# First MLP matrix as a Strassen product of seven blocks, its squares sent through DRAM to the second matrix

## The chip, the cores and the metric

One core of a Trainium2 chip runs one program that holds the whole block of the network. The metric is the time of one execution in microseconds, the median of several. The engines have the names of the profile: PE (TensorE, matmuls), DVE (VectorE), ACT (ScalarE), POOL (GpSimd) and SP (SyncE, which issues the DMAs here).

## What is computed

A diffusion block over 1,024 tokens of width 1,024: a mixer (attention beside a state-space layer), its out-projection added to x, and then the part that is changed, a modulated norm and an MLP of width 4,096 with squared ReLU. From the reference:

```python
def sq_relu_mlp(h, w1, b1, w2, b2):
    return jnp.square(jax.nn.relu(h @ w1 + b1)) @ w2 + b2
...
        x = x + g1_l * mix_l
        h2_l = modulate(rms_norm(x, norm2_g[l]), sh2_l, sc2_l)
        x = x + g2_l * sq_relu_mlp(h2_l, w_mlp1[l], b_mlp1[l], w_mlp2[l], b_mlp2[l])
```

All inputs are float32: `w_mlp1` is 1024x4096, `w_mlp2` 4096x1024. The modulation vectors come from `silu(c) @ w_mod`, of which `g2`, the gate of the MLP, is the last.

## The kernel before

**Precision.** Each float32 matrix product is made of three matmuls of a rounded type: an operand is split into a rounded part H (an ACT copy into the type fp32r) and the rest L (raw minus H, on POOL or DVE), and the products H·H, H·L and L·H are summed in one PSUM bank (`mm3`, L139–145). `wload` (L119) brings a 128x1024 block of weights into one of three raw buffers `wr`, and `wtile` (L124–137) splits it into `wH` and `wL`, four buffers each; with `scale_row` DVE first multiplies the raw block by the gate (L134). There are six PSUM banks for products (`mmc`) and two for transposes (`trc`).

**Out-projection and norm.** The loop at L1550–1579 makes x += merged @ w_out for eight token tiles, in two halves n of 512 columns. In its second half, behind the first three token tiles, stand four calls of `mod2` (L1246–1265); eight of the ten calls for one vector stream a 512 KB block of `w_mod` each, multiplied by a per-partition column on DVE (L1253, L1255) into the accumulator `m2a`; the last two add the bias and sum over partitions. `norm2(f)` (L1528) normalises tokens 512f to 512f+511 and `mod_h2` (L1539–1547) transposes them, eight groups of four 128x128 blocks, applies scale and shift, and splits into `h2H`, `h2L`.

**MLP.** Row block ft is 128 of the 4,096 hidden units. `mlp1_half(ft, w, f)` makes hidden units of ft for one half f of the tokens: 24 matmuls of 128x512 (eight contraction blocks, three terms), ReLU and square on ACT, the square again on DVE for the low part (L1607), its split on POOL (L1608). The squares stay in SBUF. `mlp1_first` runs row blocks 0 to 3 on the first half of the tokens while the second half is transposed. `mlp2(b)` multiplies the squares of two row blocks by the rows of w2, in sixteen PSUM groups of six matmuls, and DVE adds each group to x (L1645). After `mlp1_first`, `mlp1(b)` and `mlp2(b-1)` alternate. Each matrix has 1,536 matmuls of 128x512.

**Order.** The code is written in program order; the tool that builds the program puts instructions on each engine in an order of its own from the dependences and the buffers, and each engine runs its list in order. All DMAs, loads and stores, are issued by SP, in one list. A pool's tile waits for the last reader of the buffer it takes over.

Of the kernel before, what the change touches and what calls it, by code (L numbers as in the profile page):

```python
# [48 lines left out]
def block_kernel(ctx, tc, io, out, dbg=None):  # L49
# [1455 lines left out]
    x2p = ctx.enter_context(pool("x2p", reuse_waits="tile"))  # L1505
    x2 = [x2p.tile([128, 1024], F32, name=f"x2{t}") for t in range(8)]
    gb2 = x2p.tile([128, 1024], F32, name="gb2")
    LD.dma_start(gb2, bcast_rows(io["b_mlp2"], 1024))
    h2H, h2L = {}, {}

    def h2_tiles(p, f):
        for k in range(8):
            h2H[k, f] = p.tile([128, 512], F32R, name=f"h2H{k}{f}")
            h2L[k, f] = p.tile([128, 512], F32R, name=f"h2L{k}{f}")

    h2_tiles(ctx.enter_context(pool("h2a", reuse_waits="tile")), 0)
    n2 = ctx.enter_context(pool("n2", reuse_waits="tile"))
# [21 lines left out]
    def mod_h2(f, ks):  # L1539
        for k in ks:  # L1540
            p = trc()
            for i in range(4):
                T.transpose(p[:, i * 128:(i + 1) * 128], xs[4 * f + i][:, k * 128:(k + 1) * 128], ident)
            S.activation(h2H[k, f], p, AF.Identity, bias=sh2[:, k:k + 1], scale=sc2[:, k:k + 1])
            hf = n2.tile([128, 512], F32, name="hf", tag="hf", bufs=2)
            V.tensor_scalar(hf, p, sc2[:, k:k + 1], sh2[:, k:k + 1], op0=OP.mult, op1=OP.add)
            (V if k % 2 else G).tensor_tensor(h2L[k, f], hf, h2H[k, f], op=OP.subtract)

    m2_todo = list(range(20, 40))
# [60 lines left out]
    def mlp1(b):  # L1610
        for ft in (2 * b, 2 * b + 1):
            w = mlp1_tile(ft)
            for f in range(2):
                mlp1_half(ft, w, f)

    def mlp1_first():

        w = {}
        for ft in range(4):
            w[ft] = mlp1_tile(ft)  # L1620
            mlp1_half(ft, w[ft], 0)
            if ft in (1, 2):
                mod_h2(1, range(4 * ft - 4, 4 * ft))
            if ft < 3:
                for _ in range(2):
                    mod2(m2_todo.pop(0), m2a, m2r, trc)
        LD.dma_start(g2row, bcast_rows(m2_d[3], 1024))
        G.tensor_tensor(gb2, gb2, g2row, op=OP.mult)
        for ft in range(4):
            mlp1_half(ft, w[ft], 1)  # L1630
# [55 lines left out]
```

## Time and profile before

| | us |
|---|---|
| three runs, median (lowest to highest) | 1972.06 (1971.46 to 1973.39) |
| the profiled execution, its own time | 1967.57 |
| its span (first to last instruction) | 1965.6 |
| PE busy in the span | 1879.4 (96%) |
| DVE, POOL, ACT busy | 1262.6 (64%), 937.1 (48%), 641.8 (33%) |
| first MLP1 matmul, counted from the span's start | 1258.78 |
| last addition of MLP2 | 1961.96 |

The rows further below come from the one profiled execution. A busy share says how much of a stretch an engine worked; a timeline row gives start, duration, engine, line, operation, output<-inputs and, in brackets, for how long the engine had been idle before and what released it. PEclk is the granted clock of TensorE as a share of full speed, 2.4 GHz.

### The profile page before, as it was taken

How to read it: one execution, taken by the hardware profiler on the slowest of the kernel's cores; microseconds unless marked ns; L12 is line 12 of the kernel's file. 1: busy time of each engine (PE TensorE's matmuls, PEld its weight loads, DVE VectorE, ACT ScalarE, POOL GpSimd, SP SyncE). 2: the span in 40 equal slices, each digit the busy share in tenths (PEclk: the TensorE clock that was granted, in tenths of full speed). 3: DMA queues.
4: the chain of work that ended last, by engine and by line, in shares of the span. 5: the costliest groups of instructions: out<-in, count | busy, mean ns of one | idle time of the engine just before them, and what ended most of it. 6: DMA issues, size and time to landing. Idle time of an engine off the chain costs nothing.

```text
span 1965.6 us, 23750 instructions
## 1 busy us (share of the span) xinstructions
PE 1879.4 (96%) x8866; PEld 1436.1 (73%) x8866; DVE 1262.6 (64%) x2106; ACT 641.8 (33%) x980; POOL 937.1 (48%) x580
## 2 busy tenths in 40 slices
PE   7879999989899999999989999899999999999999
PEld 4667777778776555555548787778888888888887
DVE  5979999947897787777636455654344444443444
ACT  4552222244314555555551121432222211122220
POOL 2247566623335777777784442453334333334330
PEclk9989999999999999999989999999999999999999
DMA  9321222222222000000007646211111111112102
GB/s 313 80 70 49 74 62 71 75 65 69 79 73 86 17 23 23 22 23 18 23 17 247 213 135 224 65 54 43 57 51 54 43 54 44 43 43 64 44 33 86
DMA packets 144611, 144.00 MB, mean 73 GB/s; under 512 B 25648, under 2 KB 111460, under 8 KB 144496
## 3 DMA queue, kind: packets, MB, share of 16 engines
q1 hardware_dynamic: 144496, 142.48, 23.3%
q8 instruction: 70, 1.15, 0.2%
q14 instruction: 45, 0.37, 0.1%
HBM read 122.87 MB, written 19.45 MB: 72 GB/s over the span
## 4 chain that ended last, share of the span: by engine, by line
PE 66%; DVE 2%; DMA 1%; POOL 1%; issue 1%; ACT 1%; SPq 0%; DVEq 0%; ACTq 0%; POOLq 0%
PE mm L143 14%; PE mm L144 14%; PE mm L145 14%; PE pv L1194 7%; PE sT L1174 4%; PE sT L1177 4%; PE mx L1083 3%; DMA wr<-in_w_mod_dram 1%; PE mm L1560 1%; PE mm L1559 1%; PE mm L1561 1%; PE mx L1088 1%; PE mx L1218 1%; PE mm L210 1%; PE mm L211 1%; PE mm L212 1%
## 5 line engine op out<-in xcount | busy, mean ns | idle before, releaser
L136 POOL TENSOR_TENSOR wL<-wr,wH 128x1024 fp32r<-128x1024 f32 (+1 forms) x120 | 285.3, 2386 | 370.7 <-ACT wH L135 350.3
L135 ACT ACTIVATE wH<-wr 128x1024 fp32r<-128x1024 f32 (+1 forms) x124 | 126.4, 1031 | 597.8 <-PE mm L145 247.1
L1645 DVE TENSOR_TENSOR x<-x,mm 128x512 f32<-128x512 f32 x256 | 173.6, 686 | 166.2 <-PE mm L145 166.2
L1199 POOL TENSOR_TENSOR accP<-accP,P 128x1024 f32<-128x1024 f32 x96 | 240.9, 2509 | 21.0 <-ACT P L1181 15.7
L1085 DVE TENSOR_REDUCE m<-mx 128x1 f32<-128x512 f32 x240 | 154.6, 686 | 76.0 <-PE mx L1083 69.6
L1181 ACT ACTIVATE P<-sT 128x1024 f32<-128x1024 f32 x160 | 163.8, 1027 | 116.2 <-PE sT L1177 110.4
L143 PE MATMUL mm<-h2H,wH 128*128 128x512 f32 x512 | 199.5, 390 | 0.0
L144 PE MATMUL mm<-h2L,wH 128*128 128x512 f32 x512 | 199.4, 389 | 0.0
L145 PE MATMUL mm<-h2H,wL 128*128 128x512 f32 x512 | 199.4, 389 | 0.0
L143 PE MATMUL mm<-wH,sH 128*128 128x512 f32 x512 | 199.2, 389 | 0.0
L144 PE MATMUL mm<-wL,sH 128*128 128x512 f32 x512 | 199.2, 389 | 0.0
L145 PE MATMUL mm<-wH,sL 128*128 128x512 f32 x512 | 199.2, 389 | 0.0
L1608 POOL TENSOR_TENSOR sL<-r,sH 128x512 fp32r<-128x512 f32 x64 | 84.5, 1320 | 165.3 <-DVE r L1607 165.3
L134 DVE TENSOR_TENSOR wr<-wr,g2row 128x1024 f32<-128x1024 f32 x32 | 42.1, 1318 | 171.5 <-DMA wr<-in_w_mlp_dram 171.5
L1194 PE MATMUL pv<-P,Vt 128*64 128x512 f32 x640 | 150.5, 600 | 0.0
L1607 DVE TENSOR_TENSOR r<-r 128x512 f32<-128x512 f32 x64 | 89.1, 1392 | 40.7 <-ACT sH L1606 38.9
L143 PEld LDWEIGHTS mm<-h2H,wH 128*128 128x128 f32 x512 | 96.1, 188 | 20.7 <-issue 0.9
L143 PEld LDWEIGHTS mm<-wH,sH 128*128 128x128 f32 x512 | 96.1, 188 | 19.9
L144 PEld LDWEIGHTS mm<-wL,sH 128*128 128x128 f32 x512 | 96.1, 188 | 19.9
L145 PEld LDWEIGHTS mm<-wH,sL 128*128 128x128 f32 x512 | 96.1, 188 | 19.9
L145 PEld LDWEIGHTS mm<-h2H,wL 128*128 128x128 f32 x512 | 96.1, 188 | 19.8
L144 PEld LDWEIGHTS mm<-h2L,wH 128*128 128x128 f32 x512 | 96.1, 188 | 19.8
(495 smaller groups left out, 4075.2 us busy)
## 6 DMA issues: line engine op xcount, KB each, us to landing
wr<-in_w_mlp_dram SPq DMA_DIRECT2D x64, 512.0 KB
wr<-in_w_in_dram SPq DMA_DIRECT2D x35, 512.0 KB
wr<-in_w_mod_dram SPq DMA_DIRECT2D x32, 512.0 KB
x<-in_x_dram SPq DMA_DIRECT2D x12, 512.0 KB
xt<-in_w_mod_dram SPq DMA_DIRECT2D x24, 256.0 KB
gs_d<-go SPq DMA_DIRECT2D x16, 256.0 KB
q_d<-qo SPq DMA_DIRECT2D x16, 256.0 KB
ql<-q_d SPq DMA_DIRECT2D x16, 256.0 KB
```

Of the source, the lines that this page charges most:

```text
L135: S.activation(H[:, :n], raw[:, :n], AF.Copy)
L136: (low or G).tensor_tensor(L[:, :n], raw[:, :n], H[:, :n], op=OP.subtract)
L143: T.matmul(ps, lH, rH, start=i == 0, stop=False)
L144: T.matmul(ps, lH, rL, start=False, stop=False)
L145: T.matmul(ps, lL, rH, start=False, stop=i == n - 1)
L1085: V.tensor_reduce(m3[:, 4 * j + t, c:c + 1], m, axis=AX.X, op=OP.max)
L1181: S.activation(P, sT, AF.Exp, scale=HD ** -0.5)
L1194: T.matmul(pv[64 * j:64 * j + 64, :], Vt[:, kt, kv * 64:kv * 64 + 64], P[:, j * 512:(j + 1) * 512], start=kt == 0, stop=kt == NK - 1)
L1199: G.tensor_tensor(accP, accP, P, op=OP.add)
L1607: V.tensor_tensor(r, r, r, op=OP.mult)
L1608: G.tensor_tensor(sL[:, o], r, sH[:, o], op=OP.subtract)
L1645: V.tensor_tensor(x2[t][:, o], x2[t][:, o], ps, op=OP.add)
```

## The change

The change replaces the first matrix product by one with seven block products in place of eight. The 1,024 contraction rows are cut in two halves (four blocks of 128 each), and so are tokens (f = 0 and 1) and each pair of row blocks 2p, 2p+1. Of h2 transposed, B11 and B21 are the two contraction halves of the first 512 tokens and B12, B22 those of the second. The kernel makes T1 = B12 − B11, T3 = B22 − B12, T2 = B22 − T1 and T4 = B21 − T2, splits each into H and L, and multiplies each of B11, B21, T2, T1, T3, B22, T4 by a block or a sum of blocks of w1, twelve matmuls each:

- `mod_t(i)` makes B22 and T1 to T4 for contraction block i (i = 0 to 3) in place of `mod_h2(1, ...)`: two transposed groups, then two DVE operations from PSUM, seven on DVE between SBUF tiles, four on POOL and five on ACT. It is called five times, for i = 0 twice.
- `first(p)` makes the products with B11 and B21 of pair p. For p = 0 to 5 they run ahead (NA = 6), between the calls of `mod_t`.
- `mlp1(p)` makes four sums and differences of raw w1 blocks on DVE, splits them, and makes the five other products (60 matmuls; 84 for p ≥ 6, with `first(p)` inside). The four outputs are combined on DVE from PSUM.
- ReLU and square stay on ACT; the squares are stored in DRAM as float32 (`s_d`), read back and split before the second matrix, which now runs after the whole first matrix, in blocks of 1, 3 and then 4 row blocks (`BL`).
- x, stored in DRAM by `norm2` (`x2_d`), is reloaded at the hand-over into tiles that take over the buffers of the first matrix.
- The four `mod2` calls in the out-projection's second half and six behind `mlp1_first` move behind pairs 1 to 5, two each.

```diff
@@ norm2, mod_h2, mod_t
-            dump(f"x2{t}", x2[t])
+            LD.dma_start(x2_d[t], x2[t])
...
+    def mod_t(i):
+        _, b12 = h2_tr(1, i)
+        p, b22 = h2_tr(1, 4 + i)
+        H, L = BO["B22", i]
+        S.activation(H, p, AF.Identity, bias=sh2[:, 4 + i:5 + i], scale=sc2[:, 4 + i:5 + i])
+        G.tensor_tensor(L, b22, H, op=OP.subtract)
+        t1, t2, t3, t4 = (hf_tile() for _ in range(4))
+        (H1, L1), (H2, L2) = BO["B11", i], BO["B21", i]
+        V.tensor_tensor(t1, b12, H1, op=OP.subtract)
+        V.tensor_tensor(t1, t1, L1, op=OP.subtract)
+        G.tensor_tensor(t3, b22, b12, op=OP.subtract)
+        V.tensor_tensor(t2, b22, t1, op=OP.subtract)
+        V.tensor_tensor(t4, H2, t2, op=OP.subtract)
+        V.tensor_tensor(t4, t4, L2, op=OP.add)
+        for nm, t, E in (("T1", t1, G), ("T3", t3, G), ("T2", t2, V), ("T4", t4, V)):
+            H, L = BO[nm, i]
+            S.activation(H, t, AF.Copy)
+            E.tensor_tensor(L, t, H, op=OP.subtract)
...
-            if n == 1 and ts[0] < 3:
-                for _ in range(2):
-                    mod2(m2_todo.pop(0), m2a, m2r, trc)
...
+    def prod(w, h, nm):
+        ps = mmc()
+        wH, wL = w
+        for i in range(4):
+            o = slice(512 * h + 128 * i, 512 * h + 128 * i + 128)
+            bH, bL = BO[nm, i]
+            T.matmul(ps, wH[:, o], bH, start=i == 0, stop=False)
+            T.matmul(ps, wL[:, o], bH, start=False, stop=False)
+            T.matmul(ps, wH[:, o], bL, start=False, stop=i == 3)
+        return ps
...
+    def act_out(r, ft, f):
+        S.activation(r, r, AF.Square)
+        LD.dma_start(s_d[ft][:, f * 512:(f + 1) * 512], r)
+    def c_out(ps, add, ft, f):
+        r = r_tile()
+        V.scalar_tensor_tensor(r, ps, b1(ft), add, op0=OP.add, op1=OP.add)
+        S.activation(r, r, AF.Relu)
+        act_out(r, ft, f)
...
+    def first(p, w):
+        t1s[p] = ml.tile([128, 512], F32, name="t1", tag="t1", bufs=NA)
+        S.activation(t1s[p], prod(w, 0, "B11"), AF.Copy)
+        c_out(prod(w, 1, "B21"), t1s[p], 2 * p, 0)
+    def mlp1(p):
+        r1, r2 = w1_raw(2 * p), w1_raw(2 * p + 1)
...
+        if p >= NA:
+            first(p, wsplit(r1))
+        V.tensor_tensor(cs[:, a], r2[:, a], r2[:, b], op=OP.add)
+        V.tensor_tensor(cs[:, b], cs[:, a], r1[:, a], op=OP.subtract)
+        wc = wsplit(cs)
+        V.tensor_tensor(c4, r1[:, b], cs[:, b], op=OP.subtract)
+        V.tensor_tensor(r2[:, a], r1[:, a], r2[:, a], op=OP.subtract)
+        wr = wsplit(r2)
+        w4 = wsplit(c4, 512)
...
+        V.tensor_tensor(u2, prod(wc, 1, "T2"), t1s.pop(p), op=OP.add)
+        V.tensor_tensor(u4, prod(wc, 0, "T1"), u2, op=OP.add)
+        p7 = prod(wr, 0, "T3")
+        V.tensor_tensor(u3, p7, u2, op=OP.add)
+        c_out(p7, u4, 2 * p + 1, 1)
+        c_out(prod(w4, 0, "B22"), u4, 2 * p, 1)
+        c_out(prod(wr, 1, "T4"), u3, 2 * p + 1, 0)
+    mod_t(0)
+    for p in range(NA):
+        first(p, wsplit(w1_raw(2 * p)))
+        if p in (0, 2, 3):
+            mod_t((0, 0, 1, 2)[p])
+    mod_t(3)
+    m2_todo = list(range(30, 40))
+    for p in range(NP):
+        mlp1(p)
+        if 1 <= p < 6:
+            for _ in range(2):
+                mod2(m2_todo.pop(0), xs4[3], xs4[2], trc)
...
+    pre = [(s_tile(0), w2_tile(0))]
...
+    x2 = [mq.tile([128, 1024], F32, name=f"xr{t}") for t in range(8)]
+    gb2 = mq.tile([128, 1024], F32, name="gb2")
+    for t in range(8):
+        LD.dma_start(x2[t], x2_d[t])
+    LD.dma_start(gb2, bcast_rows(io["b_mlp2"], 1024))
...
+    BL = [[0], [1, 2, 3]] + [list(range(4 * b, 4 * b + 4)) for b in range(1, 8)]
+    for bi, fts in enumerate(BL):
+        tiles = pre if bi == 0 else [mlp2_tiles(ft) for ft in fts]
+        mlp2(fts, tiles, bi == len(BL) - 1)
```

How the lists of the engines move, at three places. First DVE, where the second half of the tokens is built: before, a piece of `mod_h2` between two squares.

```order
L1546 TENSOR_SCALAR hf_10943<-tr_10937,sc2_9068,sh2_9067 128x512
L1607 TENSOR_TENSOR r_10932<-r_10932 128x512
L1546 TENSOR_SCALAR hf_10952<-tr_10946,sc2_9068,sh2_9067 128x512
L1547 TENSOR_TENSOR h2L11_10839<-hf_10952,h2H11_10838 128x512
L1546 TENSOR_SCALAR hf_10961<-tr_10955,sc2_9068,sh2_9067 128x512
L1546 TENSOR_SCALAR hf_10970<-tr_10964,sc2_9068,sh2_9067 128x512
L1547 TENSOR_TENSOR h2L31_10843<-hf_10970,h2H31_10842 128x512
```

In the change, DVE's call for i = 1 (lines of the changed kernel; `hf` are the tiles b12, b22 and t1 to t4, `r` is an output of `c_out`, `wr` a raw block of w1):

```order
L1549 TENSOR_SCALAR hf_11071<-tr_11066,sc2_9068,sh2_9067 128x512
L1579 TENSOR_TENSOR T4L0_10863<-hf_10966,T4H0_10862 128x512
L1570 TENSOR_TENSOR hf_11075<-hf_11064,B11H1_10181 128x512
L1655 SCALAR_TENSOR_TENSOR r_11127<-mm_11114,cols_156,t1_11099 128x512
L1571 TENSOR_TENSOR hf_11075<-hf_11075,B11L1_10182 128x512
L1683 TENSOR_TENSOR wr_11280<-wr_11278,wr_11280 128x512
L1573 TENSOR_TENSOR hf_11076<-hf_11071,hf_11075 128x512
L1574 TENSOR_TENSOR hf_11078<-B21H1_10189,hf_11076 128x512
L1549 TENSOR_SCALAR hf_11137<-tr_11132,sc2_9068,sh2_9067 128x512
L1575 TENSOR_TENSOR hf_11078<-hf_11078,B21L1_10190 128x512
L1579 TENSOR_TENSOR T2L1_10849<-hf_11076,T2H1_10848 128x512
L1549 TENSOR_SCALAR hf_11144<-tr_11139,sc2_9068,sh2_9067 128x512
```

Eight of the twelve operations have both operands in SBUF, where three of seven had. POOL's list beside it, for the same call and up to the first operation of the next:

```order
L1572 TENSOR_TENSOR hf_11077<-hf_11071,hf_11064 128x512
L1567 TENSOR_TENSOR B22L1_10833<-hf_11071,B22H1_10832 128x512
L1579 TENSOR_TENSOR T3L1_10857<-hf_11077,T3H1_10856 128x512
L1579 TENSOR_TENSOR T1L1_10841<-hf_11075,T1H1_10840 128x512
L1663 TENSOR_TENSOR wL_11293<-wr_11280,wH_11292 128x1024
L1663 TENSOR_TENSOR wL_11297<-c4_11283,wH_11296 128x512
L1572 TENSOR_TENSOR hf_11150<-hf_11144,hf_11137 128x512
```

The splits of pair 0's weights (L1663) stand between the calls. Second, DVE in pairs 1 to 5 (`u2`, `u4` and `r` are read from PSUM, `cs`, `c4`, `wr` are sums of raw w1 blocks, L1255 is a modulation product):

```order
L1655 SCALAR_TENSOR_TENSOR r_11453<-mm_11439,cols_156,u4_11410 128x512
L1679 TENSOR_TENSOR cs_11618<-wr_11616 128x512
L1655 SCALAR_TENSOR_TENSOR r_11471<-mm_11458,cols_156,u4_11410 128x512
L1680 TENSOR_TENSOR cs_11618<-cs_11618,wr_11614 128x512
L1683 TENSOR_TENSOR wr_11616<-wr_11614,wr_11616 128x512
L1682 TENSOR_TENSOR c4_11619<-wr_11614,cs_11618 128x512
...
L1255 SCALAR_TENSOR_TENSOR xs3_10201<-wr_11722,sil_157,xs3_10201 128x1024
L1687 TENSOR_TENSOR u2_11522<-mm_11525,t1_11026 128x512
L1255 SCALAR_TENSOR_TENSOR xs3_10201<-wr_11725,sil_157,xs3_10201 128x1024
L1688 TENSOR_TENSOR u4_11524<-mm_11539,u2_11522 128x512
```

The modulation products, which wait for their weights, stand between the additions from PSUM, and the sums of pair 3's weights between the outputs of pair 1. Third, SP at the hand-over. Before, loads of w1 and w2 alternate; now it reads:

```order
L121 DMA wr_13543<-s_d_10873 128x1024
L1648 DMA s_d_10873<-r_13371 128x512
L1648 DMA s_d_10873<-r_13389 128x512
L1648 DMA s_d_10873<-r_13407 128x512
L1726 DMA xr0_13432<-x2_d_10205 128x1024
...
L1726 DMA xr7_13439<-x2_d_10205 128x1024
L1727 DMA gb2_13440<-in_b_mlp2_dram 128x1024
L121 DMA wr_13549<-in_w_mlp2_dram 128x1024
L121 DMA wr_13556<-s_d_10873 128x1024
L121 DMA wr_13562<-in_w_mlp2_dram 128x1024
```

`wr_13543` is square block 2, `wr_13549`, `wr_13556` and `wr_13562` are w2 block 2, square block 3 and w2 block 3; between them stand the last stores of squares and the reload of x.

## Rows read from the trace of the kernel before

**Rows 1.** Page, span and part 1: busy us, share, instructions by engine.

```profile
span 1965.6 us, 23750 instructions
PE 1879.4 (96%) x8866; PEld 1436.1 (73%) x8866; DVE 1262.6 (64%) x2106; ACT 641.8 (33%) x980; POOL 937.1 (48%) x580
```

**Rows 2.** Windows: stretch, us, busy PE PEld DVE ACT POOL, PEclk, DMA share, GB/s.

```profile
1300.00:1964.00 664.00, 661.92 (x2921) 547.94 (x2919) 292.55 (x346) 135.43 (x177) 238.56 (x127) 1.00 0.17 52
1500.00:1900.00 400.00, 400.00 (x1766) 331.31 (x1766) 173.47 (x204) 84.69 (x110) 149.53 (x80) 1.00 0.16 48
1180.00:1190.00 10.00, 10.00 (x46) 8.29 (x45) 3.84 (x6) 0.00 (x0) 0.00 (x0) 1.00 1.02 417
1236.00:1241.00 5.00, 5.00 (x16) 4.10 (x17) 3.22 (x6) 1.45 (x2) 0.00 (x0) 0.50 0.08 23
```

**Rows 3.** Lines by form, 1258 to 1966 us: count, busy us, mean ns, idle before.

```profile
L143 PE MATMUL mm<-h2H,wH 128*128 128x512 f32 x512 | 199.5, 390 | 0.0
...
L1645 DVE TENSOR_TENSOR x<-x,mm 128x512 f32<-128x512 f32 x256 | 173.6, 686 | 166.2 <-PE mm L145 166.2
L136 POOL TENSOR_TENSOR wL<-wr,wH 128x1024 fp32r<-128x1024 f32 x63 | 152.7, 2432 | 187.0 <-ACT wH L135 169.9 <-issue 17.0
...
L135 ACT ACTIVATE wH<-wr 128x1024 fp32r<-128x1024 f32 x61 | 63.2, 1057 | 386.6 <-PE mm L145 247.1 <-PE mm L144 110.1 <-DVE x L1645 19.0
L1604 ACT ACTIVATE r<-mm,cols 128x512 f32<-128x512 f32 x64 | 43.4, 679 | 118.2 <-PE mm L145 118.2
L134 DVE TENSOR_TENSOR wr<-wr,g2row 128x1024 f32<-128x1024 f32 x32 | 42.1, 1318 | 171.5 <-DMA wr<-in_w_mlp_dram 171.5
L1606 ACT ACTIVATE sH<-r 128x512 fp32r<-128x512 f32 x64 | 40.4, 631 | 1.9
```

**Rows 4.** Timeline, start of the MLP: first matmul, second norm, a transposed group.

```profile
1258.78 0.39 PE L143 MATMUL mm<-h2H,wH 128*128 128x512 f32 x1
...
1267.81 2.74 DVE L1536 TENSOR_SCALAR xs<-x,rs 128x1024 f32<-128x1024 f32 x4
...
1272.82 0.60 PE L1543 MATMUL tr<-ident,xs 128*128 128x128 f32 x4
```

**Rows 5.** Timeline, POOL and DVE at 1294 us.

```profile
1294.22 2.39 POOL L1628 TENSOR_TENSOR gb<-gb,g2row 128x1024 f32<-128x1024 f32 x1 [2.99 <-DMA g2row<-m_d]
...
1294.36 2.81 DVE L1607 TENSOR_TENSOR r<-r 128x512 f32<-128x512 f32 x1 [4.49 <-ACT sH L1606]
```

**Rows 6.** One line's operations: ns min/median/max, first and last start.

```profile
L1607 DVE TENSOR_TENSOR r<-r x64: 680/691/2868, 1270.5 to 1920.6; 128x512 f32<-128x512 f32 x64
...
L1547 POOL TENSOR_TENSOR h2L<-hf,h2H x8: 1255/1290/1671, 1241.1 to 1283.6; 128x512 fp32r<-128x512 f32 x8
L1547 DVE TENSOR_TENSOR h2L<-hf,h2H x8: 692/1156/1437, 1241.8 to 1283.9; 128x512 fp32r<-128x512 f32 x8
```

**Rows 7.** Timeline, second half of the out-projection: ACT, DVE, PE at 1228 to 1236.

```profile
1228.51 1.06 ACT L1532 ACTIVATE xs<-x 128x1024 f32<-128x1024 f32 x1 [4.38 <-DVE x L1564]
...
1231.74 1.29 DVE L1255 SCALAR_TENSOR_TENSOR m2a<-wr,sil,m2a 128x1024 f32<-128x1024 f32 x1 [3.26 <-DMA wr<-in_w_mod_dram]
...
1235.92 0.69 PE L1543 MATMUL tr<-ident,xs 128*128 128x128 f32 x2 [5.49 <-DVE xs L1536]
```

**Rows 8.** The chain of waits: a load of w1, start and us.

```profile
1258.26 3.86 DMA wr<-in_w_mlp_dram
```

**Rows 9.** Timeline, SP: the eight loads of x.

```profile
1173.77 5.55 SPq L1525 DMA_DIRECT2D x<-in_x_dram  x8
```

**Rows 10.** Timeline: the last addition.

```profile
1961.96 0.69 DVE L1645 TENSOR_TENSOR x<-x,mm 128x512 f32<-128x512 f32 x1 [0.67 <-PE mm L145]
```

More of the change, by code (lines that the diff above doesn't have):

```diff
@@ L1502, in block_kernel, with b_tiles @@
     man_.__exit__(None, None, None)
[L1505 to L1517, printed above, removed]
+    BO = {}
+    def b_tiles(p, names):
+        for nm in names:
+            for i in range(4):
+                BO[nm, i] = [p.tile([128, 512], F32R, name=f"{nm}{h}{i}") for h in "HL"]
+    h2a_ = pool("h2a", reuse_waits="tile")
+    b_tiles(h2a_.__enter__(), ("B11", "B21"))
+    n2_ = pool("n2", reuse_waits="tile")
+    n2 = n2_.__enter__()
     xs4 = [n2.tile([128, 1024], F32, name=f"xs{i}") for i in range(4)]
@@ L1521, in block_kernel @@
     ts2 = n2.tile([128, 8], F32, name="ts2")
-    m2a = n2.tile([128, 1024], F32, name="m2a")
-    m2r = n2.tile([128, 512], F32, name="m2r")
+    x2_d = dr.tile([8, 128, 1024], F32, name="x2_d")
+    x2p_ = pool("x2p", reuse_waits="tile")
+    x2p = x2p_.__enter__()
+    x2 = [x2p.tile([128, 1024], F32, name=f"x2{t}") for t in range(8)]
     for t in range(8):
@@ L1526, in block_kernel, with hf_tile @@
     xs = {}
+    def hf_tile():
+        return n2.tile([128, 512], F32, name="hf", tag="hf", bufs=6)
     def norm2(f):
@@ L1536, in norm2, with h2_tr, mod_h2 @@
             V.tensor_scalar(xs[t], x2[t], rs2[:, t:t + 1], None, op0=OP.mult)
-            dump(f"x2{t}", x2[t])
-    def mod_h2(f, ks):
-        for k in ks:
[L1541 to L1549, printed above, removed]
+            LD.dma_start(x2_d[t], x2[t])
+    def h2_tr(f, k):
+        p = trc()
+        for i in range(4):
+            T.transpose(p[:, i * 128:(i + 1) * 128], xs[4 * f + i][:, k * 128:(k + 1) * 128], ident)
+        hf = hf_tile()
+        V.tensor_scalar(hf, p, sc2[:, k:k + 1], sh2[:, k:k + 1], op0=OP.mult, op1=OP.add)
+        return p, hf
+    def mod_h2(ks):
+        for k in ks:
+            H, L = BO["B11" if k < 4 else "B21", k % 4]
+            p, hf = h2_tr(0, k)
+            S.activation(H, p, AF.Identity, bias=sh2[:, k:k + 1], scale=sc2[:, k:k + 1])
+            (V if k % 2 else G).tensor_tensor(L, hf, H, op=OP.subtract)
+    def mod_t(i):
[16 more added lines that the diff above has]
+            E.tensor_tensor(L, t, H, op=OP.subtract)
+    m2_todo = list(range(20, 30))
     for n in range(2):
@@ L1610, in mlp1 @@
[L1610 to L1630, printed above, removed]
@@ L1638, in mlp2 @@
+    LD.dma_start(gb2, bcast_rows(io["b_mlp2"], 1024))
+    def mlp2(fts, tiles, last_):
         for t in range(8):
```

98 lines of the change are left out of this document (59 added, 39 removed).

## The prediction

> **What bounds the kernel now.** I first read the page's busy shares: TensorE is busy 96% of the span, no other engine over 64% [rows 1]. An average over stages does not say what the MLP is worth, so next come the windows of its stretch [rows 2]: from 1300 to 1964 us TensorE works 661.9 of 664 us at clock 1.00, VectorE less than half the time, GpSimd a third, DMA a sixth. Both MLP matrices are therefore bound by TensorE, and a matmul fewer saves its whole pitch: 400 us over 1,766 matmuls are **226.5 ns** [rows 2]. The 390 ns of one in the grouped lines [rows 3] is its own length; they overlap, and the pitch counts. The groups [rows 3] give what the side engines pay: VectorE 0.69 us for a 512-wide operation from PSUM, ACT 1.06 and GpSimd 2.43 us for one 128x1024 split. Then the timelines: where the MLP begins and what its second half of tokens waits for [rows 4], and what VectorE and GpSimd do to each other there [rows 5, 6].
>
> The profiled execution takes 1967.57 us, 4.5 us less than the 1972.06 us median. My sum is made against it and moved by that 4.5. A difference of 0.2%, 3.9 us, is about what can be told from none.
>
> **The matmuls.** The first matrix goes from 1,536 matmuls to 16 pairs of 84, 1,344. 192 x 0.2265 = **-43.5 us**. The second matrix keeps its 1,536. The Trainium skill ("TensorE: Matmul & The Clock Gate", Back-to-back issue gap) states N/2.4 + 2.5 ns, 216 ns at 512 columns; by that the removed matmuls would give 41.5 us, and the sum come out 2 us higher. The row is 10 ns above the page, and I use the row. Second-half tokens are transposed in ten groups in place of eight, since the first T group is built twice: 2 x 0.6 [rows 4] = **+1.2**.
>
> **The four modulation products taken out of the out-projection's second half.** They go into pairs 1 to 5. TensorE idled 5.49 us there for the normalised x [rows 7]. ACT's last square was done at 1229.6, but VectorE's chain to it began at 1233.0 behind a product that had waited 3.26 us for its weights and ran 1.29. Without it the chain begins some 3.2 us earlier; the next five microseconds show clock 0.50 [rows 2], a loss of 2.5, part of which may go. Taken: **-5** (3 to 6).
>
> **Building the T tiles** is the price. The first B11/B21 products of six row blocks (144 matmuls) and pair 0's T2, T1, T3 (36) can run before TensorE needs T2 of the last contraction block: (144 + 36) x 0.2265 + 10 x 0.6 = 46.8 us of work. What must be done beside it: five calls, each seven VectorE operations with both operands in SBUF and four on GpSimd. The row for such a pair: VectorE's square that began 0.14 us after a GpSimd product of 2.39 us took 2.81 us in place of 0.69, ending 0.6 us behind it [rows 5, 6]; other pairs of the stretch fit too, each delayed by about the other's rest. So I add them instead of laying them side by side. An operation of VectorE holds the other up about 0.54 us (0.69 less the part that still overlaps), one of GpSimd 1.25 [rows 6] or 2.4 [rows 3]. GpSimd: 20 x 1.25 in the calls, four 1024-wide and one 512-wide weight split, 35.7 us. VectorE: 33 of the calls' 35 come before that T2, with 8 weight sums of pairs 0 and 1, 41 x 0.54, and one wide product, 0.7: 22.9. Together 58.6; with a few per cent of gaps 62. It begins when the second normalised x is there and its first groups are through: 11.8 us after the MLP's first matmul [rows 4], say 13. So T2 is ready at 75, and 75 - 46.8 = 28 us of TensorE's time are idle; with the half clock seen after an idle stretch [rows 2], 2.5, **+31**. Bounds: if the two engines did not hold each other up, VectorE alone has about 42 us of work, ready at 55, idle about 8 less what ACT and order hide: 5; with rounds of 16 us as dependences may force, 45. I take the sum since the nearest rows show the holding.
>
> **Pairs 1 to 5** have 60 matmuls, 13.6 us. VectorE owes four sums (4 x 0.65), six operations from PSUM (6 x 0.69) and in 1 to 4 two modulation products of 1.29 [rows 7], 9.3 us, with about 3.3 of holding by GpSimd 12.6. That fits, barely. There is a loop beside it: the two w1 blocks of the next pair stand on SP's queue behind the modulation weights, and with three raw buffers wait for GpSimd's split of this pair's differences. From the landing: 3.7 for the sums with their holds, 1.06 on ACT, two splits of 2.43 on GpSimd, and 3.86 for the next load [rows 8], 13.5 us, so the loop just turns in time. Taken **+1** (0 to 4). The ten pairs from 6 on have 84 matmuls, 19.0 us, against 10.4 on VectorE (seven operations from PSUM, four sums, holding 3), 8.5 on GpSimd (three splits of 1024, one of 512) and 9.6 on ACT (the same four splits, four relus of 0.68 and squares of 0.63, a copy), by the rates of [rows 3]; those cost nothing, with 8 us of cover to lose. The squares are no longer split behind the first matrix but read back and split before the second, with as many splits of 1024 for w2: a block of four row blocks asks 8 x 2.43 = 19.4 us of GpSimd beside 192 matmuls, 43.5 us. That is covered, and lost only at the start, which comes next.
>
> **The hand-over.** After the last T4 product of pair 15, 2.2 us pass in the addition, relu and square before its last square can be stored (rates of [rows 3]). Behind that store on SP's queue stand eight loads of x (512 KB), the bias, then w2 row block 2, square block 3, w2 block 3. When x came in before, it arrived at 417 GB/s [rows 2], 1.25 us each, and the eight issues took 5.55 us [rows 9]. So the twelve are in 2.2 + 2 of latency + 12 x 1.25 = 19.2 us after the last product. Then w2 block 3 still has the scale (1.32), the ACT split (1.06) and GpSimd's queue of three splits and the bias product, up to 26.6 us. Ahead of that TensorE has block 0 (48 matmuls) and of block 1 the part of its six open groups that needs no tile of these, 38 more by its order: 86, 19.5 us. Idle 7, with 2.5 for the clock after it about **+10**; the block of four behind it is ready about when TensorE comes to it, 0 to 3 more. Below 3, if the tiles before it are quicker than the queue's order says; above 20, if x's landing also holds up the first additions and their six PSUM banks. The very end is as before [rows 10].
>
> **Sum.** -43.5 + 1.2 - 5 + 31 + 1 + 10 = -5.3: 1962.3 in the profiled execution, **1966.8** by the median, called 1967.
>
> **Rivals.** (a) *The two engines hardly hold each other up*, so building costs 5 instead of 31: -5.3 - 26 = -31, **1941**. For it: in the same stretch another VectorE subtraction ran 0.69 at its best [rows 6]; against it the 2.81 [rows 5]. The Trainium skill ("SBUF — State Buffer", Who interferes with whom) says the second of such a pair waits fully until the first has ended, and by it this rival would have no chance; the 2.81 agrees.
> (b) *Pairs 1 to 5 become bound by their weights*, slower than before: the modulation products move into a stretch with 13.6 us of TensorE a pair, and each may wait for its weights on VectorE as it did before, 3.26 us [rows 7], with the pair's sums, its additions from PSUM and so the loop above queued behind. One such wait makes 13.5 into 16.8, two 20: 3.2 to 6.4 over in each of the four pairs, 13 to 26; 20 more, **1987**. The point is 13.6 us a pair, which my loop almost touches; a wait of 2 us a pair ends on the slow side. For it speaks that stores of squares, w1 and modulation weights share SP's one queue; against it that VectorE prepares a pair's weights two pairs ahead.
> (c) *The hand-over costs 22*, since the x loads, the first additions and GpSimd's splits come in line: 12 more, **1979**.
> (d) *The matmuls do not go as counted*: the count is plain in the code, and half the matmuls of the pitch's window are already in groups of six [rows 2], so products of twelve should not be slower. Were nothing saved, -5.3 + 43.5: 2010.
>
> **Chances.** Forecast 0.45 (its own range 1951 to 1983, from the 31 becoming 15 or 45 and the hand-over 10 or 12), (a) 0.22, (b) 0.20, (c) 0.11, (d) 0.02. Faster by over 3.9 us: (a) 0.22, 0.25 of the forecast's, together 0.47. Within: 0.12 of the forecast, 0.04 of (b), 0.02 of (c): 0.18. Slower: 0.08 of the forecast, 0.16, 0.09, 0.02: 0.35. The range leaves out about half of (a) below and a part of (b) above: 1944 to 1990.
>
> **What would show it.** 1,344 matmuls in the first matrix at a pitch still of 226.5; TensorE idle of 25 to 30 us between the MLP's start and T2's last split, released by VectorE's T2 subtraction; VectorE and GpSimd subtractions there at 1.2 us and more on average; an idle stretch of about 7 us at the hand-over. Wrong would be: less than 10 us idle at T2 (a), gaps in each of pairs 1 to 4 (b), or idle over 15 us after the last T4 (c).

## The result and the profile after

The changed kernel takes 1982.72 us (1981.12 to 1985.71, four runs) beside 1972.55 of the kernel before: the ratio is 1.0054 (1.0036 to 1.0071), **10 us slower**. The prediction was 1967, with 0.35 on slower by over 0.2%; the time lies in its range, the direction is wrong. The profiled execution took 1983.83 us.

The page of the changed kernel, span and part 1, beside [rows 1]:

```profile
span 1982.1 us, 23966 instructions
PE 1860.0 (94%) x8682; PEld 1413.9 (71%) x8682; DVE 1293.7 (65%) x2139; ACT 710.2 (36%) x1077; POOL 1035.8 (52%) x596
```

TensorE is busy 19 us less, though 43.5 us of matmuls are gone, and the span is 16.5 us longer: what was saved went into waits and into matmuls at the lower clock. The timeline of TensorE shows where, by the matmuls that begin and end the stages (in order: first of the out-projection, first of the MLP, last of pairs 0, 5 and 15, first and last of the second matrix):

```profile
1161.69 0.39 PE L1591 MATMUL mm<-wH,mH 128*128 128x512 f32 x1
...
1255.06 0.39 PE L1638 MATMUL mm<-B11H,wH 128*128 128x512 f32 x1
...
1343.38 0.39 PE L1640 MATMUL mm<-T4L,wH 128*128 128x512 f32 x1
...
1417.00 0.39 PE L1640 MATMUL mm<-T4L,wH 128*128 128x512 f32 x1
...
1609.43 0.39 PE L1640 MATMUL mm<-T4L,wH 128*128 128x512 f32 x1
1609.66 0.39 PE L143 MATMUL mm<-wH 128*128 128x512 f32 x1
...
1977.85 0.39 PE L145 MATMUL mm<-wH,sL 128*128 128x512 f32 x1
```

In the kernel before the out-projection begins here, and the MLP at 1258.78 [rows 4]:

```profile
1157.51 0.39 PE L1559 MATMUL mm<-wH,mH 128*128 128x512 f32 x1
```

Each stage reaches to the end of its last matmul's pitch. Beside it stands what its matmuls need at 226.5 ns, and what the prediction had beyond that:

| stage | us | matmuls at 226.5 ns | beyond them | predicted |
|---|---|---|---|---|
| out-projection to MLP (before: 101.3) | 93.4 | as before | -7.9 against before | -5 |
| build, to the end of pair 0 | 88.6 | 46.2 | 42.3, of it 6 transposes | 31 and transposes |
| pairs 1 to 5 | 73.6 | 68.0 | 5.7 | 1 |
| pairs 6 to 15 | 192.4 | 190.3 | 2.1 (four matmuls of the last modulation calls, in pair 6) | 0 |
| second matrix | 368.4 | 347.9 | 20.5 | 10 |

The whole MLP went from 703.0 to 723.0 us: its matmuls take 43.5 us less and the rest, 7.2 us before, takes 70.7. With the 7.9 ahead of it that is +12.1, near the 10.2 of the medians. (In the profile before, the out-projection began 4.2 us earlier than in the one after, which is about the distance of its time to the median.)

What TensorE waited for (waits of the changed kernel from 1255 to 1985 us; total, times, longest):

```profile
PE mm L143 <- DVE xr L1736: 9.2, 3, 4.6
PE tr L1547 <- DVE xs L1541: 4.7, 1, 4.7
PE mm L1638 <- ACT T2H L1578: 4.0, 1, 4.0
PE mm L1640 <- DVE T2L L1579: 3.9, 1, 3.9
PE tr L1547 <- ACT B22H L1566: 3.5, 2, 2.2
PE tr L1547 <- DVE hf L1549: 3.2, 1, 3.2
PE mm L1640 <- POOL T1L L1579: 3.1, 1, 3.1
PE mm L1638 <- ACT T1H L1578: 2.8, 1, 2.8
PE mm L1638 <- ACT wH L1662: 2.7, 1, 2.7
PE mm L143 <- ACT wH L1745: 2.1, 1, 2.1
PE mm L144 <- POOL wL L1746: 1.3, 1, 1.3
PE mm L1639 <- POOL wL L1663: 0.9, 1, 0.9
```

Its releasers are, in the build, the second norm (L1541), the readers of transposed groups (L1549, L1566) and the T tiles (L1578, L1579); in pairs 1 to 5 the weight splits of a pair (L1662, L1663); in the second matrix the additions to x (L1736) and the tiles' splits (L1745, L1746). They add up to 25.2 us in the build, 3.6 in the pairs and 12.6 in the second matrix, less than the 36.3, 5.7 and 20.5 lost there. The difference, 21 us, is nearly all the clock's: after most of these waits it was granted for some microseconds at the lower of its two levels (1.2 GHz, 0.50), and there matmuls begin 0.43 us apart in place of 0.23, as behind the last wait for T1:

```profile
1334.16 0.80 PE L1640 MATMUL mm<-T1L,wH 128*128 128x512 f32 x1 [3.10 <-POOL T1L L1579]
...
1335.61 0.63 PE L1638 MATMUL mm<-T2H,wH 128*128 128x512 f32 x1
1336.03 0.63 PE L1639 MATMUL mm<-T2H,wL 128*128 128x512 f32 x1
```

Windows of ten microseconds in the build, of the whole build and of block 2 of the second matrix (columns as in [rows 2]; blocks are those of `BL`):

```profile
1310.00:1320.00 10.00, 3.79 (x18) 2.36 (x16) 10.00 (x8) 4.36 (x8) 9.91 (x6) 0.73 0.07 26
1255.00:1343.00 88.00, 62.84 (x243) 48.67 (x243) 77.00 (x79) 35.67 (x56) 60.22 (x31) 0.81 0.28 89
1664.60:1708.10 43.50, 38.00 (x154) 30.51 (x153) 20.46 (x20) 7.20 (x7) 26.68 (x11) 0.92 0.36 120
```

In the build VectorE is busy 77 of 88 us and the granted clock averages 0.81, though from 1225 to 1255 us, ahead of the MLP, it was 1.00.

### The profile page after: what moved, and what is told of

It is laid out like the page before. It is cut to its first block, busy times and chain, and to the rows that moved or that the text cites. A ratio compares the mean times of both kernels' runs of the same rounds, so it can differ in the third digit from the quotient of the medians.

```text
span 1982.1 us, 23966 instructions
## 1 busy us (share of the span) xinstructions
PE 1860.0 (94%) x8682; PEld 1413.9 (71%) x8682; DVE 1293.7 (65%) x2139; ACT 710.2 (36%) x1077; POOL 1035.8 (52%) x596
## 5 line engine op out<-in xcount | busy, mean ns | idle before, releaser
L1199 POOL TENSOR_TENSOR accP<-accP,P 128x1024 f32<-128x1024 f32 x96 | 240.7, 2508 | 21.1 <-ACT P L1181 15.9
L136 POOL TENSOR_TENSOR wL<-wr,wH 128x1024 fp32r<-128x1024 f32 (+1 forms) x58 | 136.3, 2359 | 178.5 <-ACT wH L135 177.5
L1085 DVE TENSOR_REDUCE m<-mx 128x1 f32<-128x512 f32 x240 | 154.5, 686 | 76.2 <-PE mx L1083 69.7
L1736 DVE TENSOR_TENSOR xr<-xr,mm 128x512 f32<-128x512 f32 x144 | 94.5, 682 | 136.6 <-PE mm L145 129.2
L135 ACT ACTIVATE wH<-wr 128x1024 fp32r<-128x1024 f32 (+1 forms) x62 | 62.2, 1005 | 220.1 <-PE mm L144 74.6
L1663 POOL TENSOR_TENSOR wL<-wr,wH 128x1024 fp32r<-128x1024 f32 x32 | 79.7, 2493 | 88.6 <-ACT wH L1662 88.5
L1746 POOL TENSOR_TENSOR sL<-wr,sH 128x1024 fp32r<-128x1024 f32 x31 | 81.7, 2635 | 68.4 <-ACT sH L1745 68.4
L1174 PE MATMUL sT<-Q,KH 128*128 128x512 f32 x320 | 105.1, 410 | 2.2 <-ACT P L1181 2.2
L143 PE MATMUL mm<-hH,wH 128*128 128x512 f32 x248 | 101.6, 410 | 0.0
L1177 PE MATMUL sT<-Q,K 65*128 65x512 f32 x320 | 100.9, 396 | 0.0
L145 PE MATMUL mm<-hH,wL 128*128 128x512 f32 x248 | 98.4, 397 | 0.0
L144 PE MATMUL mm<-hL,wH 128*128 128x512 f32 x248 | 98.4, 397 | 0.0
```

Source lines behind the costliest of these rows:

```text
L136: (low or G).tensor_tensor(L[:, :n], raw[:, :n], H[:, :n], op=OP.subtract)
L143: T.matmul(ps, lH, rH, start=i == 0, stop=False)
L144: T.matmul(ps, lH, rL, start=False, stop=False)
L145: T.matmul(ps, lL, rH, start=False, stop=i == n - 1)
L1085: V.tensor_reduce(m3[:, 4 * j + t, c:c + 1], m, axis=AX.X, op=OP.max)
L1174: T.matmul(o, KH[kv][:, ks], Q1[:, j], start=True, stop=False)
```

## The experiments

Stage times of all runs, read as above, each from one profile; medians of the kernel before stood at 1970.5 to 1971.6 in these runs, and at 1972.55 beside the changed kernel, so times of two rows compare to a microsecond or two.

| run | build | pairs 1 to 5 | 6 to 15 | second matrix | time, us |
|---|---|---|---|---|---|
| changed kernel | 88.6 | 73.6 | 192.4 | 368.4 | 1982.72 |
| e1, T0 once | 77.2 | 69.3 | 192.4 | 368.0 | 1966.35 |
| e2, calls on VectorE | 81.2 | 74.3 | 192.4 | 368.7 | 1976.26 |
| e3, modulation late | 88.5 | 68.0 | 201.0 | 367.4 | 1984.67 |
| e4, bias late | 88.7 | 73.4 | 192.4 | 362.9 | 1980.31 |
| e5, order of x | 88.6 | 73.5 | 192.4 | 361.1 | 1975.81 |
| e6, modulation spread | 88.7 | 68.0 | 192.8 | 368.2 | 1977.91 |
| e11, no reload | 88.8 | 75.8 | 192.4 | 363.6 | 1975.71 (one) |
| e8, rebuilt | 62.0 | 71.9 | 192.8 | 359.3 | 1945.22 |
| e10, rebuilt 2 | 64.7 | 70.2 | 192.8 | 360.2 | 1948.97 |
| e12, rebuilt 3 | 60.9 | 69.8 | 192.8 | 359.4 | 1942.15 |

### The build: e1 and e2

```diff
-        if p in (0, 2, 3):
+        if p in (2, 3):
```

> The T group of contraction block 0 is built once instead of twice; nothing else changes. Theory (the build is the sum of what VectorE and GpSimd hold each other up for): a call costs seven times 0.54 and four times 1.25 us, near 9, with its operations from PSUM up to 13; the stretch from the first MLP1 matmul to the last of pair 0, 88.6 us in the changed kernel, falls to 76 to 80, the time by 9 to 13 us. Rival (TensorE waits for something else there, the transposes or the raw weights): it falls by less than 4.

The build fell by 11.3 us, as the theory had it. The time fell by 16.4: pairs 1 to 5 lost 4.3 us of their stall as well, which was not expected. VectorE's first weight sums of pairs 2 to 5 come 2.5 to 4.8 us earlier there, counted from the end of pair 0 (pair 4's 28.8 us after it in place of 31.3), so the loop of loads that is shown below had more lead; why it had is open.

```diff
-        G.tensor_tensor(L, b22, H, op=OP.subtract)
+        V.tensor_tensor(L, b22, H, op=OP.subtract)
...
-        G.tensor_tensor(t3, b22, b12, op=OP.subtract)
+        V.tensor_tensor(t3, b22, b12, op=OP.subtract)
...
-        for nm, t, E in (("T1", t1, G), ("T3", t3, G), ("T2", t2, V), ("T4", t4, V)):
+        for nm, t, E in (("T1", t1, V), ("T3", t3, V), ("T2", t2, V), ("T4", t4, V)):
```

> The four GpSimd operations of each T call (512 wide) run on VectorE. Theory (the two engines take turns): each of the 20 gives back 1.25 us of turn and takes 0.69, with the 0.5 that a GpSimd operation itself waits; T2's last part is ready 5 to 12 us earlier than the 77.9 after the first MLP1 matmul, and the time falls by 4 to 10 us. Rival (VectorE is simply full there, its records show 10.0 busy of 10 us): 20 operations more of 0.69 to 1.2, 12 to 24 us later, and the time rises by that.

More work on the engine that was busy throughout, and the build is 7.3 us shorter, the time 6.5. The changed kernel's timelines of VectorE and GpSimd show the taking of turns:

```profile
1312.12 1.75 DVE L1679 TENSOR_TENSOR cs<-wr 128x512 f32<-128x512 f32 x1
1313.80 1.75 DVE L1573 TENSOR_TENSOR hf<-hf 128x512 f32<-128x512 f32 x1
```

```profile
1311.61 1.71 POOL L1572 TENSOR_TENSOR hf<-hf 128x512 f32<-128x512 f32 x1
1313.29 1.71 POOL L1567 TENSOR_TENSOR B22L<-hf,B22H 128x512 fp32r<-128x512 f32 x1
```

One operation of each goes through every 1.68 us, and both records read 1.7, of which part is waiting; the prediction had added 0.54 and 1.25, 1.79. The Trainium skill ("SBUF — State Buffer", Who interferes with whom) has the second of two such operations wait for the whole of the first; the turns agree, but for some 0.25 us by which each pair is shorter than 0.68 and 1.25 together. VectorE's splits of T2 (ns min/median/max) in the changed kernel and then in e2:

```profile
L1579 DVE TENSOR_TENSOR T2L<-hf,T2H x5: 677/1745/2851, 1279.4 to 1331.2; 128x512 fp32r<-128x512 f32 x5
```

```profile
L1579 DVE TENSOR_TENSOR T2L<-hf,T2H x5: 678/685/692, 1281.6 to 1316.6; 128x512 fp32r<-128x512 f32 x5
```

Without GpSimd beside it, each takes 0.68 us. The last T2 is begun at 1316.6, 59.2 us after this run's first MLP1 matmul (1257.4), where it was 76.2 (1331.2 less 1255.1): 17 us earlier, more than the 5 to 12 expected. Of these only 7.3 arrive, because pair 0's weight sums now stand behind it in VectorE's list, and TensorE waits for them (waits of e2):

```profile
PE mm L1638 <- ACT wH L1662: 18.2, 3, 16.4
```

### Pairs 1 to 5: e3 and e6

VectorE's first weight sum of each pair (L1679), the changed kernel's timeline:

```profile
1346.49 0.69 DVE L1679 TENSOR_TENSOR cs<-wr 128x512 f32<-128x512 f32 x1 [0.22 <-DMA wr<-in_w_mlp_dram]
...
1359.55 0.69 DVE L1679 TENSOR_TENSOR cs<-wr 128x512 f32<-128x512 f32 x1 [1.88 <-DMA wr<-in_w_mlp_dram]
...
1374.66 1.07 DVE L1679 TENSOR_TENSOR cs<-wr 128x512 f32<-128x512 f32 x1 [2.69 <-DMA wr<-in_w_mlp_dram]
...
1390.88 0.69 DVE L1679 TENSOR_TENSOR cs<-wr 128x512 f32<-128x512 f32 x1 [3.46 <-DMA wr<-in_w_mlp_dram]
```

These are the sums of pairs 2 to 5. They come 13.1, 15.1 and 16.2 us apart, against 13.6 of TensorE: the loop of loads falls behind, and pair 5's sum waits 3.46 us for its load. The one stall of these pairs, at 1395 us in pair 4, follows from that by the order of the lists. TensorE wants the split of pair 4's `c4` (the wait of 2.7 for L1662). VectorE had made `c4` by 1378.3, but its split stands in ACT's list behind a relu, whose input stands in VectorE's list behind the waiting sum (VectorE's timeline, then ACT's):

```profile
1392.82 0.74 DVE L1655 SCALAR_TENSOR_TENSOR r<-mm,cols,u 128x512 f32<-128x512 f32 x1
```

```profile
1393.59 0.63 ACT L1656 ACTIVATE r<-r 128x512 f32<-128x512 f32 x1 [11.13 <-DVE r L1655]
...
1394.79 0.61 ACT L1662 ACTIVATE wH<-c 128x512 fp32r<-128x512 f32 x1
```

```diff
-        if 1 <= p < 6:
+        if 6 <= p < 11:
```

> The ten modulation calls stand behind pairs 6 to 10 instead of 1 to 5, where a pair has 19.0 us of TensorE work. Theory (the loop of raw buffers, loads and VectorE's waits for modulation weights runs at 15 to 16 us a pair against 13.6): pairs 1 to 5 take 68 us in place of 73.6, no stall in pair 4, no new one in 6 to 10; 4 to 6 us less. Rival (the loads of w1 and the stores of squares alone make the loop too slow): the stall stays, within 2 us.

Half right. Pairs 1 to 5 take 68.0 us, no stall left; but two of pairs 6 to 10 take 4 us more each, and the time is not better (ratio 1.0072, 1.0057 to 1.0088, beside the changed kernel's 1.0054). The waits and VectorE's timeline of e3 show what a wide pair's 19 us did not cover:

```profile
PE mm L1638 <- DVE u L1687: 4.1, 2, 2.2
```

```profile
1451.81 2.46 DVE L1255 SCALAR_TENSOR_TENSOR xs<-wr,sil,xs 128x1024 f32<-128x1024 f32 x1 [3.36 <-DMA wr<-in_w_mod_dram]
1454.20 0.68 DVE L1687 TENSOR_TENSOR u<-mm,t 128x512 f32<-128x512 f32 x1
```

A modulation product waits 3.36 us for its weights, and TensorE waits for the addition from PSUM behind it.

```diff
-        if 1 <= p < 6:
-            for _ in range(2):
-                mod2(m2_todo.pop(0), xs4[3], xs4[2], trc)
+        if 1 <= p < 11:
+            mod2(m2_todo.pop(0), xs4[3], xs4[2], trc)
```

> One modulation call behind each of pairs 1 to 10 instead of two behind 1 to 5. Theory (four raw loads a pair through three buffers are what is too slow, in narrow and in wide pairs): with three loads a pair no pair stalls; pairs 1 to 5 take 68 to 69 us instead of 73.6 and pairs 6 to 15 no more than 192.5; 4 to 6 us less. Rival (one modulation product on VectorE, waiting for its weights, is enough): stalls of 2 to 4 us in some pairs between 4 and 10.

As the theory had it: no pair stalls, and the time falls by 4.8 us. So two modulation calls a pair are too much and one is not. The edit takes a load and a VectorE product out of a pair together, so it does not show that the fourth load through three buffers alone is the cause.

### The hand-over: e4, e5 and e11

Against the matmuls' own pitch the second matrix of the changed kernel is behind by 5.6 us after 48 matmuls (block 0), 11.3 after 96 and 11.3 at the end of block 1, 20.3 before the last 48 of block 2, and 20.5 at the end of the matrix. The first 5.6 us begin with a wait of 3.7 at 1617.6 for the additions of block 0, of which VectorE's first had waited for x:

```profile
1616.87 6.28 DVE L1736 TENSOR_TENSOR xr<-xr,mm 128x512 f32<-128x512 f32 x10 [6.20 <-DMA xr<-x_d]
```

The next 5.7 begin with the waits for tiles of block 1 (L1745, L1746), after 66 and 71 matmuls; the last of these, the split of w2 block 2, ended 25.6 us after the last T4 product. The loss of block 2 is the additions' (timelines in block 2, of VectorE, GpSimd and SP):

```profile
1694.60 2.36 DVE L1753 TENSOR_TENSOR wr<-wr,g2row 128x1024 f32<-128x1024 f32 x1 [6.76 <-DMA wr<-in_w_mlp_dram]
1696.89 3.66 DVE L1736 TENSOR_TENSOR xr<-xr,mm 128x512 f32<-128x512 f32 x6
```

```profile
1685.53 3.37 POOL L1764 TENSOR_TENSOR xr<-xr,gb 128x1024 f32<-128x1024 f32 x1
1688.86 2.39 POOL L1746 TENSOR_TENSOR sL<-wr,sH 128x1024 fp32r<-128x1024 f32 x1
```

```profile
1691.28 0.33 SPq L121 DMA_DIRECT2D wr<-in_w_mlp_dram  x1
```

Six additions from PSUM stand behind a scale of w2 that waits 6.76 us for its load, and TensorE waits for them (4.6 us, the longest wait of L1736); the load is issued at 1691.28, as GpSimd's split ends that frees its raw buffer, and that split stood behind an addition of the bias.

```diff
-        if 2 <= bi < 6:
-            for t in (2 * bi - 4, 2 * bi - 3):
+        if 4 <= bi < 8:
+            for t in (2 * bi - 8, 2 * bi - 7):
```

> GpSimd's additions of the gated bias to x stand two blocks later in the second matrix. Theory (the stall 78 to 88 us into the second matrix comes since VectorE's additions from PSUM stand behind a scale of w2 whose load waits for a raw buffer, which GpSimd frees late because of two bias additions of 3.4 and 2.3 us): the stall with its low clock, 8.8 us, falls to 3 or less; 5 to 9 us less. Rival (splits, loads and scales make that loop too slow without them too): within 3 us.

In the profile the loss of block 2 falls from 9.0 to 3.1 us and the second matrix by 5.5. The medians show 2.4, within the 3 of its rival and not clear of the noise (ratio 1.0050, 1.0034 to 1.0066): the stall is shown to depend on the bias additions by the profile alone.

```diff
+    for t in range(4):
+        LD.dma_start(x2[t], x2_d[t])
...
+    tiles1 = [mlp2_tiles(ft) for ft in BL[1]]
+    for t in range(4, 8):
+        LD.dma_start(x2[t], x2_d[t])
+    LD.dma_start(gb2, bcast_rows(io["b_mlp2"], 1024))
```

> At the hand-over four of the eight loads of x and the bias are issued behind the loads of w2 block 2, square block 3 and w2 block 3 instead of ahead of them. Theory (these tiles are late because 4.7 MB of x and bias go before them): the two stalls 23 to 26 us into the second matrix, 4.2 us with 1.5 of low clock, go; the second matrix takes 363 to 365 us instead of 368.4. The first stall, for x itself, stays. Rival (the tiles are bound by raw buffers and GpSimd's splits): within 1.5 us of 368.4.

The time falls by 6.9 us, but not by the way expected. After 96 matmuls the kernel is 11.4 us behind, as before the edit: the early loss only moved, from the tiles to the additions of x. Gone is the loss of block 2, 0.8 us instead of 9.0. The scale that waits is still there, for 6.93 us and with seven additions behind it, but it begins 80.5 us into the second matrix in place of 84.9: the tiles' chain of loads runs some 4 us earlier.

```diff
-        LD.dma_start(x2[t], x2_d[t])
+        V.memset(x2[t], 0.0)
```

> The changed kernel with the eight reloads of x at the hand-over left out (the tiles are set to zero on VectorE instead, so x is missing from the output). Theory (the hand-over's 20.5 us come from the 4 MB of x in SP's queue: the first additions wait for it, and the tiles of block 1 land behind it): the stall at the start and those 23 to 26 us into the second matrix go, the one at 78 to 88 may shrink; 352 to 360 us instead of 368.4. Rival (the squares' way through DRAM and their split on GpSimd are what is late): the stalls at 23 to 26 us stay, 364 or more.

Neither. The eight settings (0.91 us each) stand on VectorE ahead of the first addition, so they took the reload's place: TensorE waits 6.0 us there. The tiles are late again (waits of e11, 1606 to 1710 us):

```profile
PE mm L143 <- DVE xr L1736: 6.0, 1, 6.0
PE mm L144 <- POOL wL L1746: 4.6, 2, 2.9
```

That says little about the rival: block 1's scales of w2 begin only at 1625.95, behind the sixteen additions that the settings had delayed, and GpSimd idles 4.3 us before its split at 1626.2. What the reload alone costs stays open. The loss of block 2 is gone here too.

### The wait ahead of the MLP: e7 and e9

```diff
-            if n == 1 and ts[0] < 3:
-                for _ in range(2):
-                    mod2(m2_todo.pop(0), m2a, m2r, trc)
...
-            if ft < 3:
-                for _ in range(2):
-                    mod2(m2_todo.pop(0), m2a, m2r, trc)
+            for _ in range(3 if ft < 2 else 2):
+                mod2(m2_todo.pop(0), m2a, m2r, trc)
```

> The kernel before, with its four modulation calls of the out-projection's second half moved behind the first row blocks of the MLP (ten there instead of six): that part of the change alone. Theory (TensorE waited there for VectorE, held by a modulation product): the first MLP1 matmul comes 3 to 5 us earlier, the MLP itself as long as before (703 us); 3 to 5 us less, up to 9 if the median of the kernel before stands 4.5 us above its profile for this reason. Rival (the calls cost in the MLP what they save before it): within 2 us.

1971.99 us against 1971.17, ratio 0.9999 (0.9988 to 1.0009): nothing. The edit did not do what it says: the building tool drew the calls forward into the same place. VectorE's timeline there:

```profile
1235.43 1.28 DVE L1255 SCALAR_TENSOR_TENSOR m2a<-wr,sil,m2a 128x1024 f32<-128x1024 f32 x1 [3.28 <-DMA wr<-in_w_mod_dram]
1236.63 0.16 DVE L1533 TENSOR_SCALAR ss<-ss 128x4 f32<-128x4 f32 x1
```

In the changed kernel the accumulator is a tile of the norm, so they cannot be drawn forward. e9 therefore leaves the products out:

```diff
-    m2_todo = list(range(20, 40))
+    m2_todo = list(range(20, 31)) + [38, 39]
...
-            if n == 1 and ts[0] < 3:
-                for _ in range(2):
-                    mod2(m2_todo.pop(0), m2a, m2r, trc)
```

> The kernel before with seven of the eight products of its last modulation vector (the MLP's gate) left out, so that none stands on VectorE in the out-projection's second half; the rest is computed. Theory (TensorE's wait for the normalised x is VectorE held by a product that waits for its weights): from the first out-projection matmul to the first of the MLP 93 to 98 us pass, as in the changed kernel (93.4), in place of 101.3, and the wait of 5.5 us falls under 2. Rival (the chain of the norm itself is too long there, and the changed kernel only has another order of matmuls): 100 to 101, the wait stays over 4.

93.6 us from the out-projection to the MLP, and no wait; 1963.0 us in its one run beside 1970.6, and the MLP as long as before (702.9). VectorE's chain begins as soon as ACT's square is there:

```profile
1230.25 0.17 DVE L1533 TENSOR_SCALAR ss<-ss 128x4 f32<-128x4 f32 x1 [1.22 <-ACT xs L1532]
```

So 7.7 us of the kernel before (101.3 less 93.6) hung on these products, with no Strassen in it.

### All repairs: e8, e10 and e12

```diff
+    for p in range(NA):
+        first(p, wsplit(w1_raw(2 * p)))
+        if 1 <= p < 5:
+            mod_t(p - 1)
+        if p == 3:
+            ws0 = prep(0)
...
+        _, b12 = h2_tr(1, i, True)
```

(with the edits of e2, e4, e5 and e6; `prep` is the first half of `mlp1`, and `True` makes b12 on ACT)

> All repairs together: the T group of block 0 once; the calls' GpSimd operations on VectorE, and b12 from PSUM on ACT; the calls behind row blocks 1 to 4 of the run-ahead, pair 0's weight sums behind block 3; one modulation call a pair; bias additions two blocks later; the loads of x in two halves. Theory (the build is VectorE's and GpSimd's turns, 4 x 8.4 us on VectorE alone now, from 12 us after the first MLP1 matmul on): T2 is ready 47 to 50 us after it, TensorE hardly waits, pair 0 ends after 52 to 60 us instead of 88.6; with the other repairs 1935 to 1950. Rival (what is gained at the build returns as stalls in the pairs, whose lead came from it): over 1955.

1945.22 us, ratio 0.9863 (0.9848 to 0.9878): **26 us faster than the kernel before**. The last T2 is ready 54 us after the first MLP1 matmul, not 47 to 50, and the build takes 62.0 instead of 52 to 60. What TensorE still waits for there (1254 to 1350 us) are mostly splits of weights:

```profile
PE mm L1642 <- POOL wL L1666: 4.5, 3, 1.8
...
PE mm L1641 <- ACT wH L1665: 1.8, 2, 1.5
```

> The rebuilt version, with pair 0's weight sums behind run-ahead block 4 instead of 3, and the modulation calls behind pairs 3 to 12 instead of 1 to 10. Theory (in the rebuilt version blocks 3 and 4 of the run-ahead waited for raw buffers that pair 0 held, and pair 1 for a load behind the first modulation weights): build to the end of pair 0 55 to 60 us instead of 62.0, pairs 1 to 5 68 to 69 instead of 71.9; 4 to 9 us less than 1945. Rival (pair 0's weights then come too late and take their place): within 2.

Missed: pair 0's weights behind block 4 cost the build 2.7 us more, and only the later modulation calls gave back 1.7 in the pairs; the time, 3.8 us more than e8's, is outside what the rival had too. e12 keeps the latter alone:

```diff
-        if 1 <= p < 11:
+        if 3 <= p < 13:
```

> The rebuilt version (pair 0's weight sums behind run-ahead block 3 again), with the modulation calls behind pairs 3 to 12 instead of 1 to 10. Theory (pair 1's stall of 3.9 us was a load of w1 behind the first modulation weights): pairs 1 to 5 take 68 to 69 us instead of 71.9, the rest stays; 2 to 4 us less than 1945. Rival (the load is late without them): within 1.

Pairs 1 to 5 take 69.8 us, 2.1 less; pair 1 still stalls for 1.8, so only half of its stall went with the modulation calls. 1942.15 us, ratio 0.9853 (0.9824 to 0.9882), the best of all, though its interval and that of e8 overlap.

## Why the prediction was wrong

**The matmuls.** Right: 192 fewer, and twelve to a product keep the pitch: a narrow pair took 13.60 us without a stall, a wide one 19.04, 226.7 ns a matmul. The 216 ns that the Trainium skill gives ("TensorE: Matmul & The Clock Gate", Back-to-back issue gap) for a matmul by itself are 10 ns under both; the 131 ns that the section gives for a stream of weight loads and matmuls is seen in neither.

**The modulation calls ahead of the MLP.** Right in kind, -5 for -7.9; e9 gives 7.7 for the products alone.

**Building the T tiles.** That the two engines hold each other up was right and is shown by e2; e1 (a call less, 11.3 us) fits its price. Rival (a) is out. T2 was ready at 77.9 us (forecast 75), from this row of VectorE's timeline and the MLP's start at 1255.06:

```profile
1331.24 1.75 DVE L1579 TENSOR_TENSOR T2L<-hf,T2H 128x512 fp32r<-128x512 f32 x1
```

(GpSimd's 35.7 in the sum add up to 36.0 by its rows; nothing hangs on it.) But nothing waited for that last T2: the last T1 came from GpSimd 1.2 us later (the wait until 1334.16). And the idle time was not one wait. It was 11.4 us in the transposes, 7.9 at T2 and 5.9 at T1, together 25.2 for the 28 forecast. The loss was 36.3 (88.6 less 46.2 and 6.0 of transposes) for 31, since the low clock after these waits cost 11.1, where the sum had "with the half clock seen after an idle stretch [rows 2], 2.5". This term was mis-sized: it was taken once for the stage.

**Pairs 1 to 5.** "So the loop just turns in time. Taken +1" was 5.7: 3.6 of waiting and 2.1 of low clock, all in pair 4. The loop of 13.5 us was near the 13.1 of the first pair, but later ones took up to 16.2, and e3 and e6 show that the modulation calls did it. This is rival (b) in a mild form, 4.7 us instead of 20.

**The hand-over is the step that failed.** Its first part came out in size, +10 forecast and 11.3 measured up to the end of block 1, but by luck. 5.6 of it were lost at additions that waited for x, which the sum had left out. TensorE then wanted tiles after 66 matmuls, not 86. And the tile it waited for was w2 block 2's, ready after 25.6 us; block 3's, for which the sum had "up to 26.6" (the terms named for it add up to 31.3 at 2.43 for each of GpSimd's four operations), came after 30.3, and nothing waited for it. e5 shows that with the tiles earlier the additions of x cost as much. Then "the block of four behind it is ready about when TensorE comes to it, 0 to 3 more" was 9.0, and I had taken 0. I asked only when tiles would be ready. What stopped TensorE were additions behind a waiting scale in VectorE's list, in the very block whose tiles had been ready. So the second matrix lost 20.5, almost the 22 of rival (c), but block 2's 9.0 by another mechanism than the loads of x.

The misses add up: 9.0 + 1.3 at the hand-over, 4.7 in the pairs, 5.3 in the build, less 2.9 ahead of the MLP, 17.4: -5.3 becomes +12.1. (The 2.1 us of pair 6 and the last 0.2 of the second matrix have their like in the 7.2 us that the MLP lost before.) Cut the other way, the build, the pairs and the second matrix idled 41.4 us for 36 forecast, and the low clock cost 21.1 (11.1, 2.1 and 7.9) for 5. So two terms failed: the 0 for the block of four, and the clock, counted once for the build and once for the hand-over.

## What to carry to other kernels

A saving of matmuls is only worth what the engines beside TensorE can prepare in the time that is left; first count what the new tiles need of VectorE and GpSimd together, and where their operations with both inputs in SBUF meet, add them. An engine's list is in order, so an operation that waits for a load also holds up the evictions behind it: look for it in the blocks after the one that is being filled. It was so in three places here: block 2, pair 4 and the wide pairs of e3. And where waits of TensorE come in pieces, count the low clock behind each, not once for a stage. The same algorithm went from 10 us slower to 28 us faster by one repeated call left out and the rest moved in order or to another engine, and 7.9 of the 28 came from four calls that had nothing to do with it.

## What was not expected of the hardware

Moving work onto an engine that read 10 of 10 us busy made the stage shorter: its records held the waits for the other engine (1.75 us for 0.68 of work), so a full engine by the page need not be full. And the lower clock after many short waits cost half as much as the waits themselves, 21 us beside 41.
